# A diffusion block's first modulation, from column sums to products with a spread SiLU row, and its Fourier blocks four products side by side

## The chip, the cores and the metric

The kernel runs on one core of a Trainium2 chip. The metric is the device time of one execution in microseconds (us), as the median of the runs of a kernel. TensorE is called PE here, VectorE DVE, ScalarE ACT, GpSimd POOL, and SyncE, which issues most of the loads and stores, SP. Each engine works through its own list of instructions in order; a later one never overtakes one that waits.

## What is computed

One layer over 2048 latent tokens of width 1024 and 256 context tokens. What matters here is its beginning:

```python
sh1, sc1, g1, sh2, sc2, g2 = split(silu(c) @ w_ada + b_ada)      # w_ada: 1024 x 6144
hx = rms_norm(x, norm1_g) * (1 + sc1) + sh1                       # 2048 x 1024
fx, qx, kx, vx = split(hx @ w_in)                                 # fx: 512 columns, "Fourier"
y_four = fourier_mix(fx)                                          # needs every token
gates = sigmoid(hx @ w_branch_gate)                               # 2048 x 2048
# then attention, gated merge, output projection, and the squared-ReLU MLP
```

A product in 32-bit precision is made of three PE products of halves: each operand is split in a high part and a low part, and high-high, high-low and low-high are added in one PSUM bank (`mm3`, line 80). From the second quarter of the tokens on the halves are 16-bit numbers, scaled by powers of two.

## The kernel before, in words

The tokens are worked on in quarters j = 0 to 3 of 512. The width of 1024 is cut in KT = 8 blocks k of 128 channels. Weights come in units of 256 columns. The list `seq` (line 724) orders the work on PE in pairs of units: first the two Fourier units f, then two gate units g, then query, value, key and gate units. In pair 0 the output of quarter j of a unit is two products of 24 matmuls each (`unit_T`, line 535: 8 blocks by 3 products of halves), with 512 tokens in the free direction. The results are written to DRAM (`put_T`, line 530). The instructions of every engine are put in order when the program is built, by a scheduler that is held to a certain order only where the code says `issue_after`.

**The modulation.** AB (line 134) holds for each block k one column of shifts and one of scales, with a channel on each partition. `ada_load` (line 265) brings, per block, 1 MB of w_ada: input channels on the partitions, 128 shift and 128 scale columns side by side. `ada_sum` (line 272) multiplies input block after input block by the SiLU of c (a number per partition, `sil`) and adds them on DVE: two scalings (L278), then multiply-adds (L280), then an addition of two partial sums (L281). For blocks from 2 on, DVE takes six of the eight input blocks (PE_K = 6, line 737) and PE the other two. `ada_cols` (line 284) then sums over the partitions by PE products with a column of ones (L292), and with `sil` for those two (L291); DVE adds the bias (L294) and applies the norm gain (L295).

**Quarter 0** is built with 32-bit halves, since the power of two by which hx is scaled (`norm_scale`, line 249) is known only when all eight blocks of AB are there. `load_x` (line 194) fetches 128 tokens, squares them (L203 on ACT, L201 on DVE), raises the mean to the power -1/2 on POOL (L175) and scales the tokens (L208, L206). `hx_k` (line 211) transposes a block of 512 tokens on PE (L217), evicts it twice on ACT with AB's columns as scale and bias (L220, L222: firstH and ht) and has DVE make the low half (L225). The loop at line 768 makes block k + 1 and then the 12 products of block k, four output banks side by side. The weights' 32-bit halves are made by `split_on` (line 88: L90, L93).

**Quarters 1 to 3.** `build` (line 227) does the same with 16-bit halves: transposes (L233), ht (L237 on DVE or L239 on ACT), high half (L240), low half (L241). `load_unit` (line 495) finds the norm of a weight unit (L504, L505, L510, L511 to L515) and makes its halves (L523, L524). In pair 0, `run_pair` (line 802) works quarter 1, 2, 3. Between the two units of a quarter it calls `first_tokens` (line 789, quarter 0's 32-bit halves into 16-bit ones: L796, L798, L799) and fetches, normalises and builds the next quarter. All four quarters of hx stay in SBUF, in four rooms of one tag (line 697). Beside later products, `tick` (line 473) steps through side work, the other columns of the modulation first, and `load_gains` and `load_rope` (lines 547 and 564) fetch norm gains and rotary tables, which POOL multiplies (L571).

The rooms are shared. In the beginning, the weights of modulation lie in rooms that later hold hx and the rotary tables.

Of the kernel before, what the change touches and what calls it, by code (L numbers as in the profile page):

```python
# [8 lines left out]
F32 = mybir.dt.float32  # L9
# [57 lines left out]
def dit_block(ctx: ExitStack, tc: tile.TileContext, a, out, taps=None, upto=9):  # L67
# [126 lines left out]
    def load_x(src, r0, name, xh=None, sq_on_dve=False, scale_on_dve=False):  # L194
        if xh is None:
            xh = pb.tile([128, D], F32, tag="xh", name=f"xh_{name}", bufs=5)
        load(xh, src[r0:r0 + 128, :])
        sq = pb.tile([128, D], F32, tag="xsq", name=f"xsq_{name}")
# [6 lines left out]
        if scale_on_dve:  # L205
            dve.tensor_scalar(out=xh, in0=xh, scalar1=rs, scalar2=None, op0=ALU.mult)  # L206
        else:
            act.activation(xh, xh, AF.Copy, scale=rs)  # L208
        return xh

    def hx_k(xhs, k, hx, ab, name, t_on_act=False):

        hH, hL = hx
        w = hH.shape[2]
        tp = tpp.tile([128, 512], F32, tag="tp", name=f"tp_{name}_{k}")[:, :w]
# [3 lines left out]
        t = pb.tile([128, 512], F32, tag="ht", name=f"ht_{name}_{k}", bufs=2)[:, :w]  # L219
        h_ = act.activation(hH[:, k, :], tp, AF.Identity, bias=bi, scale=sc)  # L220
        if t_on_act:
            act.activation(t, tp, AF.Identity, bias=bi, scale=sc)  # L222
        else:
            dve.tensor_scalar(out=t, in0=tp, scalar1=sc, scalar2=bi, op0=ALU.mult, op1=ALU.add)
# [24 lines left out]
    def norm_scale(ab, i, name):  # L249
# [13 lines left out]
        dve.tensor_scalar(out=ab, in0=ab, scalar1=hsc[:, 2 * i:2 * i + 1], scalar2=None, op0=ALU.mult)  # L263
# [20 lines left out]
    def ada_cols(dst, j, c0, gain, name, acc, wt=None, nk=KT):  # L284

        ps = adp.tile([128, 512], F32, tag="ad", name=f"ad{name}")
        for i in range(2):
            bs = slice(i * 128, (i + 1) * 128)

            for k in range(nk, KT):  # L290
                pe.matmul(ps[:, i:i + 1], wt[:, k, bs], sil[:, k:k + 1], start=(k == nk), stop=False)  # L291
            pe.matmul(ps[:, i:i + 1], acc[:, bs], ones[:, 0:1], start=(nk == KT), stop=True)  # L292
        b = 32 + c0 // 128
        dve.tensor_tensor(out=view(dst, j, [[8, 2]]), in0=ps[:, 0:2], in1=view(vecT, b, [[8, 2]]), op=ALU.add)  # L294
        dve.scalar_tensor_tensor(out=dst[:, 8 + j:9 + j], in0=dst[:, 8 + j:9 + j], scalar=1.0, in1=gain,  # L295
                                 op0=ALU.add, op1=ALU.mult)

    def side_work():
        for dst, d0, s0, g0, o in ((ABc, 0, 8, 16, "c"), (AB2, 3 * D, 0, 24, "m")):
            for k in range(KT):  # L300
                c0 = d0 + k * 128
                acc = ada_sum(ada_load(k + (8 if d0 else 0), f"{o}{k}"), s0, f"{o}{k}")
                yield
                ada_cols(dst, k, c0, vecT[:, g0 + k:g0 + k + 1], f"{o}{k}", acc)
# [385 lines left out]
    sp.dma_start(vec[0:8, :], a["c"].rearrange("o (k p) -> (o k) p", p=128))  # L690
    sp.dma_start(vec[8:16, :], a["c_ctx"].rearrange("(k p) -> k p", p=128))
    sp.dma_start(vec[16:24, :], a["norm1_g"].rearrange("o (k p) -> (o k) p", p=128))
    sp.dma_start(vec[24:32, :], a["norm2_g"].rearrange("o (k p) -> (o k) p", p=128))
    sp.dma_start(vec[32:80, :], b_ada.rearrange("o (k p) -> (o k) p", p=128))
# [1321 lines left out]
```

## Time and profile before

| what | us |
|---|---|
| median of 3 runs | 2602.69 (2600.85 to 2606.18) |
| the profiled execution's own time | 2595.27 |
| its span, first to last instruction | 2593.5 |
| PE busy in the span | 2509.0 |
| PE busy from 0 to 157.4 (up to the first gate product) | 122.48 |
| PE busy from 157.4 to 900 | 716.92 |
| PE busy from 900 to 1700 | 781.94 |
| PE busy from 1700 to the end | 887.70 |

The profile is of one execution. Busy times overlap between engines, and matmuls overlap with each other, so that a busy time is not a price. A row of the timeline has its start, its length, the engine, the line of the kernel, the operation with the tiles written and read, shapes, and in brackets how long the engine was idle before it and what ended that. An x and a number behind a row say how many instructions are merged in it. In the list of groups the mean length of one instruction follows the busy time.

### The profile page before, as it was taken

What the parts mean: (1) busy time and instruction counts of PE and PEld (TensorE: products, weight loads), DVE (VectorE), ACT (ScalarE), POOL (GpSimd) and SP (SyncE); (2) the same over time, 40 slices, a digit from 0 to 9 for tenths busy, and PEclk for the clock granted to TensorE, in tenths of its full rate; (3) what the DMA queues carried; (4) which work ended last, traced back from release to release, by engine and by line L of the source; (5) the groups of instructions that cost most, each with busy time, mean ns of one, the idle gap of its engine ahead of it and who ended that gap; (6) DMA issues with size and microseconds to landing.
All of it is one profiled execution on the core that took longest, in us unless ns stands there. A gap on an engine that the chain in (4) does not pass through costs nothing.

```text
span 2593.5 us, 42160 instructions
## 1 busy us (share of the span) xinstructions
PE 2509.0 (97%) x15842; PEld 1445.0 (56%) x15842; DVE 1800.7 (69%) x3735; ACT 1199.8 (46%) x2118; POOL 450.7 (17%) x561
## 2 busy tenths in 40 slices
PE   7899999999999899999999999999999999999999
PEld 5445666777655577786665444444444444444444
DVE  7656969655464788986775887979778534546367
ACT  5633255335644688983444655546360423223150
POOL 1200221012122456620000121121212000000000
PEclk9899999999999999999999999999999999999999
DMA  7465666545875576646667777776876433333334
GB/s 276 119 217 203 200 212 235 188 157 191 288 282 159 143 229 191 188 142 202 233 217 273 256 264 241 256 259 228 287 269 196 141 95 109 97 107 94 110 102 154
DMA packets 223125, 506.39 MB, mean 195 GB/s; under 512 B 31732, under 2 KB 85756, under 8 KB 207816
## 3 DMA queue, kind: packets, MB, share of 16 engines
q1 hardware_dynamic: 189960, 384.57, 45.8%
q0 software_dynamic: 26176, 87.90, 9.6%
q10 hardware_dynamic: 6784, 31.21, 3.6%
q8 instruction: 124, 2.03, 0.3%
q14 instruction: 81, 0.66, 0.1%
HBM read 366.22 MB, written 137.38 MB: 194 GB/s over the span
## 4 chain that ended last, share of the span: by engine, by line
PE 74%; DVE 9%; DMA 9%; ACT 4%; issue 3%; SPq 1%; POOL 1%; ACTq 0%; DVEq 0%; POOLq 0%
PE p L85 20%; PE pm L85 19%; PE ps_g L85 8%; PE po L85 6%; PE pua L85 3%; PE tp L1444 2%; PE ps_q L85 2%; PE ps_f L85 2%; DMA vt<-v 2%; PE ps_v L85 2%; PE pv L1458 2%; PE ps_k L85 2%; DMA w12m<-in_w_mlp 2%; PE pmf L1379 1%; DMA w12m<-in_w_mlp1t 1%
## 5 line engine op out<-in xcount | busy, mean ns | idle before, releaser
L85 PE MATMUL pm<-hc,wb 128*128 128x512 f16 x2688 | 582.6, 379 | 5.5 <-DVE u L1728 3.5
L85 PE MATMUL p<-wb,a 128*128 128x512 f16 x2688 | 581.9, 379 | 2.4 <-DVE X L1853 1.8
L85 PEld LDWEIGHTS <-wb 128*128 128x128 f16 x2688 | 263.0, 98 | 323.4 <-issue 7.2
L85 PEld LDWEIGHTS <-a 128*128 128x128 f16 x2688 | 263.0, 98 | 320.0 <-issue 3.2
L85 PE MATMUL ps_g<-hx,w_g 128*128 128x512 f16 x1536 | 343.7, 379 | 0.0
L1853 DVE SCALAR_TENSOR_TENSOR X<-p,msc,X 128x512 f32<-128x512 f32 x280 | 201.5, 747 | 157.8 <-PE p L85 139.3
L85 PEld LDWEIGHTS <-hx 128*128 128x128 f16 x2304 | 227.0, 99 | 39.3 <-issue 3.6
L85 PEld LDWEIGHTS <-w_g 128*128 128x128 f16 x1536 | 150.4, 99 | 165.4 <-issue 0.9
L85 PE MATMUL po<-wo,mH 128*128 128x512 f16 x512 | 152.4, 379 | 0.0
L1728 DVE TENSOR_TENSOR u<-pm,u 128x512 f32<-128x512 f32 x128 | 87.4, 689 | 84.3 <-PE pm L85 82.5
L404 ACT ACTIVATE wo<-ws,msc 128x512 f16<-128x512 f32 x96 | 69.0, 719 | 161.4 <-DVE ws L446 130.2
L1732 ACT ACTIVATE p<-pm 128x512 f32<-128x512 f32 x32 | 18.9, 589 | 239.3 <-PE pm L85 239.3
L1431 DVE CUSTOM_DVE_ANT_0 s<-sc,bt,qsc 128x736 f32<-128x736 f32 (+5 forms) x128 | 111.2, 869 | 21.3 <-PE sc L1425 15.6
L1452 DVE SCALAR_TENSOR_TENSOR pL<-tp,pH 128x640 f16<-128x640 f32 (+1 forms) x128 | 112.4, 878 | 11.4 <-ACT pH L1447 10.7
L1864 POOL DMA_DIRECT2D xr<-x1d x32 | 17.2, 538 | 569.7 <-DVE X L1728 562.8
L1435 ACT ACTIVATE s<-s,m 128x736 f32<-128x736 f32 (+5 forms) x128 | 104.6, 817 | 15.1 <-DVE m L1431 15.0
L532 ACT ACTIVATE ot_g<-ps_g,usc_g 128x512 f32<-128x512 f32 x64 | 43.7, 683 | 146.2 <-PE ps_g L85 139.4
L1444 PE MATMUL tp<-ident,s 128*128 128x128 f32 x704 | 102.5, 280 | 4.1 <-ACT s L1435 3.9
L404 ACT ACTIVATE wo<-raw,msc 128x512 f16<-128x512 f32 x128 | 87.8, 710 | 38.1 <-DVE raw L446 17.0
L405 DVE SCALAR_TENSOR_TENSOR wo<-raw,msc,wo 128x512 f16<-128x512 f32 x128 | 94.3, 746 | 10.7 <-ACT wo L404 10.6
L85 PE MATMUL po<-wo,mL 128*128 128x512 f16 x256 | 97.0, 379 | 0.0
L1447 ACT ACTIVATE pH<-tp 128x640 f16<-128x640 f32 (+1 forms) x128 | 95.9, 749 | 0.5 <-PE tp L1444 0.5
(574 smaller groups left out, 4376.3 us busy)
## 6 DMA issues: line engine op xcount, KB each, us to landing
wb<-w1d SPq DMA_DIRECT2D x224, 256.0 KB
wb<-w2d SPq DMA_DIRECT2D x224, 256.0 KB
raw<-in_w_mlp ACTq DMA_DIRECT2D x24, 1024.0 KB
w1d<-wo POOLq DMA_DIRECT2D x84, 256.0 KB, 3.8
w2d<-wo POOLq DMA_DIRECT2D x84, 256.0 KB, 4.0
gT<-ot_g SPq DMA_DIRECT2D x64, 256.0 KB
w12m<-in_w_mlp1t SPq DMA_DIRECT2D x16, 1024.0 KB
w12m<-in_w_mlp SPq DMA_DIRECT2D x16, 1024.0 KB
```

What stands on the lines that cost most here:

```text
L85: last_mm[0] = pe.matmul(ps, l, r, start=(start and i == 0), stop=(stop and i == n - 1))
L404: act.activation(hi, src, AF.Copy, scale=scale)
L405: dve.scalar_tensor_tensor(out=lo, in0=src, scalar=scale, in1=hi, op0=ALU.mult, op1=ALU.subtract)
L532: last_out[0] = act.activation(o, ps, func, scale=scale)
L1431: tail["dve"] = dve.tensor_tensor_reduce(out=s[:, :n], in0=sc, in1=bias, op0=ALU.add, op1=ALU.min, scale=qsc[:, 4:5], scalar=3.0e38, accum ...
L1435: tail["act"] = act.activation(s[:, :n], s[:, :n], AF.Exp, bias=m1[:, 0:1], scale=-1.0, accum_out=m1[:, 1:2])
L1444: tail["pe"] = pe.transpose(tp[:, i * 128:(i + 1) * 128], s[:, o:o + 128], ident)
L1447: tail["act"] = act.activation(pH[:, :c], tp[:, :c], AF.Copy, scale=PTOP)
L1452: tail["dve"] = dve.scalar_tensor_tensor(out=pL[:, :c], in0=tp[:, :c], scalar=PTOP, in1=pH[:, :c], op0=ALU.mult, op1=ALU.subtract)
L1458: tail["pe"] = pe.matmul(pv, p_[:nk, i * 128:(i + 1) * 128], vv[:nk, h2 * 128 + o:h2 * 128 + o + 64], start=(j == 0 and i == 0), stop=(j = ...
L1728: last["dve"] = dve.tensor_tensor(out=o, in0=x, in1=y, op=op)
L1853: last["dve"] = dve.scalar_tensor_tensor(out=X[x], in0=ps, scalar=down if op == ALU.subtract else up, in1=X[x], op0=ALU.mult, op1=ALU.add)
```

## The change

- **The first modulation.** w_ada's first 2048 columns also come transposed (`w_ada_t`): an output channel on each partition, its 1024 weights along the lane, shift and scale side by side, 1 MB per block as before. ACT spreads `sil` to 1024 columns, PE transposes it in eight pieces and ACT copies it back, so that every partition has the whole SiLU row (`silb`). `first_channels` now needs two DVE instructions per block that multiply a lane by that row and sum (the profile's name of such an instruction is that of L201), each with a short read of the sum, and the two small ones on AB. Column sums on PE are gone for this modulation. The other modulations keep them, with another order of columns.
- **The start.** One load of a packed `vec` takes the place of five. The four x tiles of quarter 0 are fetched ahead of modulation block 0; `load_x` is parted in `x_fetch` and `x_norm`. The tokens of quarter 1 lie in rooms of their own (`x1_rooms`), those of quarter 3 in rooms that the SiLU row and a first weight half leave.
- **The order in pair 0.** The f weights' norms and high halves are made beside the first products (`f_norm`, `f_part`). `quad` makes a quarter's four products side by side, block after block, 12 matmuls each, in all four PSUM banks. hx of the next quarter (`steps`) and quarter 0's 16-bit halves (`first_tokens`) are made block by block beside it. hx has a named room for each quarter; quarter 3's is the one that held quarter 0's 32-bit low halves, and quarter 0's halves are made in the rooms of the modulation and copied by two DMAs of 1 MB into the room of its 32-bit high halves.

The core of the diff:

```diff
+    silw = silb[:, D:2 * D].rearrange("p (k n) -> p k n", n=128)
+    with tc.issue_after(exp_.ins):
+        spread_ = act.activation(silw, view(sil, 0, [[1, KT], [0, 128]]), AF.Copy)
...
+        for k in range(4):
+            pe.transpose(ps[:, k * 128:(k + 1) * 128], silw[:, 4 * h + k], ident)
+        with tc.issue_after(scaled[0].ins):
+            act.activation(silb[:, h * 512:(h + 1) * 512], ps, AF.Copy)
...
     def first_channels(k):
-        if k + 1 < KT:
-            first_sums(k + 1)
-        ada_cols(AB, k, k * 128, vecT[:, 16 + k:17 + k], f"s{k}", sums[k], first_ada[k], PE_K if k > 1 else KT)
-        made.append(hx_k(xhs, k, hx32, AB, "00", True))
...
+        with after(chan[-1], made[k - 2][1]) if k > 1 else nullcontext():
+            acc = pb.tile([128, 2], F32, tag="acc2", name=f"acc{k}", bufs=2)
+            for o in range(2):
+                w = first_ada[k][:, o * D:(o + 1) * D]
+                dve.tensor_tensor_reduce(out=w, in0=w, in1=silb[:, 0:D], op0=ALU.mult, op1=ALU.add, scale=1.0, scalar=0.0, accum_out=acc[:, o:o + 1])
+            dve.tensor_tensor(out=view(AB, k, [[8, 2]]), in0=acc, in1=view(vecT, 32 + k, [[8, 2]]), op=ALU.add)
...
+    def steps(j, room, xh):
+        hx[j] = room = room or hx_room(j, f"hx{j}")
+        for k in range(KT):
...
+            if k % (2 if j == 1 else 4):
+                dve.tensor_scalar(out=t, in0=tp, scalar1=sc, scalar2=bi, op0=ALU.mult, op1=ALU.add)
+            else:
+                act.activation(t, tp, AF.Identity, bias=bi, scale=sc)
+            edge["act"] = act.activation(room[:, 0, k], t, AF.Copy)
+            edge["dve"] = dve.tensor_tensor(out=room[:, 1, k], in0=t, in1=room[:, 0, k], op=ALU.subtract)
+            yield
...
+        hx[0] = room = hx_room(2, "hx0")
+        for o in range(2):
+            sp.dma_start(room[:, o].rearrange("p k t -> p (k t)"), r[o].rearrange("p k t -> p (k t)"))
+        yield
...
+    def quad(j, beside):
+        units = list(zip(f_w, f_usc))
+        ps = [mmp.tile([128, 512], F32, tag="mm", name=f"ps_f{m}_{j}") for m in range(4)]
+        for k in range(KT):
+            for m in range(4):
+                w, ms = units[m // 2][0], slice((m % 2) * 128, (m % 2 + 1) * 128)
+                mm3(ps[m], [(w[:, 0, k, ms], w[:, 1, k, ms], hx[j][:, 0, k], hx[j][:, 1, k])], k == 0, k == KT - 1)
+            beside(k)
         for m in range(4):
+            put_T(ps[m], fT, m, j * 512, AF.Copy, f"f{m}_{j}", units[m // 2][1][:, 1:2], o=f_room(m, f"ot_f{m}_{j}"))
...
+        def beside2(k):
+            if k == 0:
+                norm_quad(3, x_last)
+            if k < 3:
+                next(tokens)
+                next(tokens)
+            if k == 3:
+                for _ in tokens:
+                    pass
+            if k >= 4:
+                next(b3)
+                next(b3)
```

How the instructions stand now, at two places. On DVE, in the middle of the modulation, before: `aaccs` are the partial sums, `ads` PE's column sums, `sparec` and `sparer` rooms of w_ada.

```order
L278 TENSOR_SCALAR aaccs_344<-sparec,sil 128x256 x2
L280 SCALAR_TENSOR_TENSOR aaccs_344<-sparec,sil,aaccs_344 128x256 x2
L294 TENSOR_TENSOR AB<-ads_352,vecT 128x2
L280 SCALAR_TENSOR_TENSOR aaccs_344<-sparec,sil,aaccs_344 128x256 x2
L295 SCALAR_TENSOR_TENSOR AB<-AB,vecT 128x1
L281 TENSOR_TENSOR aaccs_344<-aaccs_344 128x256
L278 TENSOR_SCALAR aaccs_383<-sparer,sil 128x256 x2
L280 SCALAR_TENSOR_TENSOR aaccs_383<-sparer,sil,aaccs_383 128x256 x3
L225 TENSOR_TENSOR firstL<-ht_3_366,firstH 128x512
```

The same engine and place now, `ISA` being the product with a sum and, with 128x1, the reading of the sum; rooms 153 to 156 are named `hx_room` from the start.

```order
L773 ISA hx_room_153,acc_315<-hx_room_153,silb 128x1024
L773 ISA acc_315 128x1
L773 ISA hx_room_153,acc_315<-hx_room_153,silb 128x1024
L773 ISA acc_315 128x1
L229 TENSOR_TENSOR hx_room_156<-ht_2_293,hx_room_155 128x512
L774 TENSOR_TENSOR AB<-acc_315,vecT 128x2
L775 SCALAR_TENSOR_TENSOR AB<-AB,vecT 128x1
L773 ISA sparer,acc_376<-sparer,silb 128x1024
L773 ISA acc_376 128x1
```

AB of a block now follows its sums on the same engine, where before it took them from PE one block later.

On ACT, from the outputs of the quarter 1 products (`ot_f`) to the first high half of quarter 2 (`hx_822`), before; `xh` are quarter 2's tokens.

```order
L532 ACTIVATE ot_f_0_734<-ps_f_0_709,usc_f_592 128x512
L532 ACTIVATE ot_f_1_762<-ps_f_1_737,usc_f_592 128x512
L532 ACTIVATE ot_f_0_920<-ps_f_0_895,usc_f_608 128x512
L203 ACTIVATE xsq_784,ss_785<-xh_782 128x1024
L532 ACTIVATE ot_f_1_948<-ps_f_1_923,usc_f_608 128x512
L203 ACTIVATE xsq_794,ss_795<-xh_792 128x1024
L208 ACTIVATE xh_782<-xh_782,rs_789 128x1024
L208 ACTIVATE xh_792<-xh_792,rs_799 128x1024
L203 ACTIVATE xsq_1015,ss_1016<-xh_1013 128x1024
L208 ACTIVATE xh_1013<-xh_1013,rs_1020 128x1024
L239 ACTIVATE ht_0_828<-tp_0_823,AB 128x512
L240 ACTIVATE hx_822<-ht_1_837 128x512
```

On ACT now, from the outputs of quarter 2 (`ot_f_2`) to the first high half of quarter 3 (`hx_1002`); `t_4` to `t_7` and `h0H` are quarter 0's last blocks.

```order
L534 ACTIVATE ot_f_2_1119<-ps_f_2_873,usc_f_356 128x512
L534 ACTIVATE ot_f_2_1122<-ps_f_2_874,usc_f_356 128x512
L897 ACTIVATE h0H<-t_4_943 128x512
L534 ACTIVATE ot_f_2_1125<-ps_f_2_875,usc_f_366 128x512
L897 ACTIVATE h0H<-t_5_948 128x512
L534 ACTIVATE ot_f_2_1128<-ps_f_2_876,usc_f_366 128x512
L895 ACTIVATE t_6_965<-hx_room_156,hsc 128x512
L895 ACTIVATE t_7_970<-hx_room_156,hsc 128x512
L897 ACTIVATE h0H<-t_6_965 128x512
L897 ACTIVATE h0H<-t_7_970 128x512
L883 ACTIVATE ht_0_1008<-tp_0_1003,AB 128x512
L884 ACTIVATE hx_1002<-ht_0_1008 128x512
```

The next quarter's squares and scalings no longer stand behind the outputs, but quarter 0's last blocks do, and ahead of these twelve rows stand two norms of gate weights, with t_4 and t_5 between them.

More of the change, by code (lines that the diff above doesn't have):

```diff
@@ L282, in ada_sum, with ada_cols @@
         return acc[:, 0, :]
-    def ada_cols(dst, j, c0, gain, name, acc, wt=None, nk=KT):
+    def ada_cols(dst, i, d0, g0, name, acc):
         ps = adp.tile([128, 512], F32, tag="ad", name=f"ad{name}")
[L287 to L296, printed above, removed]
+        for h in range(2):
+            pe.matmul(ps[:, h:h + 1], acc[:, h * 128:(h + 1) * 128], ones[:, 0:1], start=True, stop=True)
+        scale, j = i < 4, 2 * (i % 4)
+        o = dst[:, 8 + j:10 + j] if scale else dst[:, j:j + 2]
+        b = 32 + d0 // 128 + (8 if scale else 0) + j
+        dve.tensor_tensor(out=o, in0=ps[:, 0:2], in1=vecT[:, b:b + 2], op=ALU.add)
+        if scale:
+            dve.scalar_tensor_tensor(out=o, in0=o, scalar=1.0, in1=vecT[:, g0 + j:g0 + j + 2], op0=ALU.add, op1=ALU.mult)
     def side_work():
@@ new lines, in dit_block @@
+    ada_rooms = [wide[i][:, o:o + 2048] for i in (1, 0) for o in (0, 2048)]
+    ada_rooms.append(pb.tile([128, 2, 16, 64], F32, tag="rcos", name="sparer").rearrange("p o t d -> p (o t d)"))
+    ada_rooms += ada_rooms[:3]
+    silb = pb.tile([128, 2, KT, C], F16, tag="hc", name="silb").bitcast(F32).rearrange("p o k t -> p (o k t)")
+    def first_load(k):
+        load(ada_rooms[k], a["w_ada_t"][k])
+        return ada_rooms[k]
+    w_in = a["w_in"]
+    w_g = a["w_branch_gate"]
+    raw_f = [pa.tile([128, KT, 256], F32, tag="wst", name=f"ws_f{u}", bufs=2) for u in range(2)]
@@ L780, in dit_block @@
[L780 to L800 removed]
+            with after(*made[1]):
+                first_half(1)
@@ new lines, in dit_block @@
+        if k == 2:
+            for i in range(5, 8):
+                first_ada[i] = first_load(i)
+            xh = [x_fetch(x2, (4 + i) * 128, f"01{i}", x1_rooms[i // 2][:, i % 2 * D:(i % 2 + 1) * D]) for i in range(4)]
+            x_late = fetch_quad(2)
+        first_products(k)
+        if k == 2:
+            with after(*made[3]):
+                for u in range(2):
+                    f_norm(u)
+        if k in (4, 5):
+            with after(made[k][0]):
+                f_part(k - 4, False)
@@ new lines, in dit_block, with f_room @@
+    x_last = fetch_last()
+    ordered[0] = False
+    for i, t in enumerate(xh):
+        with after(*made[5 if i < 2 else 6]):
+            x_norm(t, f"01{i}", i == 3, i == 3)
+    with after(norm_scale(AB, 0, "x"), made[7][1]):
+        f_part(0, True)
+    for u in f_usc:
+        dve.tensor_tensor(out=u[:, 1:2], in0=u[:, 5:6], in1=hsc[:, 1:2], op=ALU.mult)
+    def f_room(i, name):
+        if i % 2:
+            return pb.tile([128, 2, 512], F16, tag="s" + "HL"[i // 2], name=name, bufs=2).bitcast(F32).rearrange("p a t -> p (a t)")
```

237 lines of the change are left out of this document (155 added, 82 removed).

## The prediction

> **What bounds the kernel now.** First the page, for the share of each engine.
>
> ```profile
> span 2593.5 us, 42160 instructions
> ...
> PE 2509.0 (97%) x15842; PEld 1445.0 (56%) x15842; DVE 1800.7 (69%) x3735; ACT 1199.8 (46%) x2118; POOL 450.7 (17%) x561
> ```
>
> TensorE (PE) is busy for 97% of the span, so only its idle time can be won, and most of that lies where the change is made. The view by windows shows it for the stretch up to the first gate product. Its columns are the window, its length, then busy time and instructions of each engine, granted clock, DMA share and GB/s.
>
> ```profile
> 0.00:10.00 10.00, 0.37 (x1) 0.18 (x1) 3.21 (x12) 2.55 (x4) 1.00 (x11) 1.00 0.64 238
> 10.00:20.00 10.00, 3.77 (x12) 2.09 (x12) 4.63 (x13) 8.93 (x13) 3.19 (x4) 1.00 1.03 403
> 20.00:58.00 38.00, 36.74 (x199) 31.44 (x199) 33.86 (x94) 18.86 (x26) 4.77 (x5) 0.96 0.72 288
> ...
> 87.00:101.00 14.00, 4.97 (x18) 3.04 (x19) 7.79 (x16) 10.05 (x15) 4.70 (x5) 0.59 0.19 67
> ...
> 124.00:137.00 13.00, 6.91 (x43) 4.23 (x42) 11.27 (x19) 7.63 (x11) 10.58 (x5) 1.00 1.02 297
> ...
> sum 157.51, PE 122.59 PEld 76.19 DVE 109.53 ACT 88.30 POOL 29.59; mean PE 13.62 PEld 8.47 DVE 12.17 ACT 9.81 POOL 3.29
> ```
>
> PE is idle for 157.51 - 122.59 = 34.9 us there: 15.9 before 20 us, 9.0 in 87 to 101, 6.1 in 124 to 137. The list of PE's waits names the last two and part of the first:
>
> ```profile
> PE tp L233 <- ACT xh L208: 7.6, 2, 6.4
> PE ads L292 <- DVE aaccs L281: 6.9, 1, 6.9
> ...
> PE ps_f L85 <- DVE hx L241: 4.2, 1, 4.2
> ```
>
> The middle row is the start (the first column sum), the first is the token block of quarter 2, normalised only after quarter 1's outputs, the third quarter 3's block, late on VectorE (DVE). Between 20 and 58 PE looks busy but runs 96 exact products and 32 transposes in 37 us. The PE timeline (start, length, instruction) gives the marks against which I count:
>
> ```profile
> 20.34 2.07 PE L85 MATMUL ps_first<-firstH,w_first 128*128 128x512 f32 x4 [0.92 <-ACT firstH L220]
> ...
> 62.56 1.04 PE L85 MATMUL ps_f<-hx,w_f 128*128 128x512 f16 x4 [1.36 <-ACT w_f L523]
> ...
> 83.67 2.75 PE L85 MATMUL ps_f<-hx,w_f 128*128 128x512 f16 x12
> ...
> 136.98 4.00 PE L85 MATMUL ps_f<-hx,w_f 128*128 128x512 f16 x10 [4.25 <-DVE hx L241]
> ...
> 157.37 2.97 PE L85 MATMUL ps_g<-hx,w_g 128*128 128x512 f16 x13
> ```
>
> So the first products start at 20.3, quarter 1 runs from 62.6 to 86.4, and gate products begin at 157.4. From the gate products on, PE's list is the same products in the same order in both kernels: what is won or lost before 157.4 is the forecast, provided that nothing behind it waits anew.
>
> **The start.** One vector load replaces five, and the four x tiles stand ahead of the first modulation load.
>
> ```profile
> 0.72 0.40 SPq L690 DMA_DIRECT2D vec<-in_c  x1
> ...
> 2.18 0.32 SPq L694 DMA_DIRECT2D vec<-in_b_ada  x1
> ...
> 3.95 0.37 PE L711 MATMUL pvec<-ident,vec 80*128 80x80 f32 x1 [3.95 <-DMA vec<-in_b_ada]
> ...
> 5.37 0.17 DVE L717 TENSOR_TENSOR sil<-e,vecT 128x16 f32<-128x16 f32 x1
> ```
>
> The last of the five was taken 3.95 - 2.18 = 1.8 us after its issue, so the single one is there at 2.5 and the SiLU at 4.1 (5.54 - 3.95 = 1.6 later). In the chain of waits the first modulation block (1 MB) came 5.05 us after its issue:
>
> ```profile
> 2.54 5.05 DMA spare<-in_w_ada
> ```
>
> At the 403 GB/s of 10 to 20 us 1 MB takes 2.6, so 2.45 of it is latency. In the new order x tiles land at about 5.0, 6.3, 7.6, 8.9, modulation block 0 at 11.5, the first weight halves at 12.8 and 14.1, and then 2.6 us for each modulation block (the last at 34.8, before its turn). The prices of what is done with them, from the list of groups (count, busy us and mean ns, idle before):
>
> ```profile
> L241 DVE TENSOR_TENSOR hx<-ht,hx 128x512 f16<-128x512 f32 x24 | 16.8, 725 | 2.7 <-ACT hx L240 2.6
> ...
> L240 ACT ACTIVATE hx<-ht 128x512 f16<-128x512 f32 x24 | 14.4, 627 | 3.4 <-DVE ht L237 3.2
> ...
> L208 ACT ACTIVATE xh<-xh,rs 128x1024 f32<-128x1024 f32 x8 | 9.1, 1143 | 5.0 <-POOL rs L175 4.9
> ...
> L280 DVE SCALAR_TENSOR_TENSOR aaccs<-spare,sil,aaccs 128x256 f32<-128x256 f32 x20 | 8.4, 479 | 0.0
> ...
> L203 ACT ACTIVATE xsq<-xh 128x1024 f32<-128x1024 f32 x7 | 7.4, 1050 | 6.1 <-DMA xh<-in_x 6.1
> ...
> L220 ACT ACTIVATE firstH<-tp,AB 128x512 fp32r<-128x512 f32 x8 | 6.2, 776 | 18.2 <-DVE AB L295 18.1
> ...
> L201 DVE CUSTOM_DVE_ANT_0 xsq<-xh 128x1024 f32<-128x1024 f32 x5 | 6.1, 1225 | 0.2 <-DMA xh<-in_x 0.2
> L225 DVE TENSOR_TENSOR firstL<-ht,firstH 128x512 fp32r<-128x512 f32 x8 | 5.5, 688 | 0.3 <-ACT ht L222 0.3
> ...
> L93 DVE TENSOR_TENSOR w_first<-ws_f,w_first 128x1024 fp32r<-128x1024 f32 x4 | 4.9, 1222 | 3.1 <-ACT w_first L90 3.1
> ...
> L504 ACT ACTIVATE usq_f<-ws_f 128x2048 bf16<-128x2048 f32 x2 | 3.8, 1910 | 0.9 <-DVE ss L201 0.9
> ```
>
> A mean overlaps its neighbour by about 0.1, so I count 1.05 for a square, 1.1 for a scaling or a half of weights, 0.55 for a 512-wide copy, 1.9 for a weight norm. ScalarE (ACT): spread 4.1 to 5.2, two squares, two scalings, two copies of the row, 11.0. DVE: two squares and two scalings of x, 11.7; two product-sums (no such shape with the spread row stands in the trace; the nearest is L201, same size, 1225 ns, and I take that) 2.45 and two small ones 0.4: channel block 0 at 14.6. ACT's second weight half ends at 15.1, firstH 0.78 later: first product at **15.9**, 4.4 us sooner. The spread and its eight transposes cost PE nothing, since it idles there.
>
> **The eight channel blocks.** Before, one cost DVE two scalings, four L280 (six in the first two) and an addition, 0.6 + 4 x 0.42 + 0.4 = 2.7, with firstL 3.3; then came column sums on PE between its products, and DVE again: that trip is why ACT's L220 waited 18.1 us for AB. Now it is 2.45 + 0.4 + 0.62 for firstL = 3.5 on DVE, a little more, but without the trip. Block 1 comes late, behind two low halves (1.22 each) and firstL: 14.6 + 2.45 + 0.6 + 2.9 = 20.6. Block 2 waits for ACT's two evictions, firstL and the other two low halves: 28.4. Then 31.9, 35.4, 39.0, and with the small operations of the weight norm and the scale between them 43.0 and 46.8. Before, the last stood at 54.5:
>
> ```profile
> 54.50 0.16 DVE L295 SCALAR_TENSOR_TENSOR AB<-AB,vecT 128x1 f32<-128x1 f32 x1
> ```
>
> **Quarter 1.** From block 5 (39.0) on, ACT's queue is the bound, since squares and weight halves now stand between the evictions: 1.45 (evictions of block 5) + 2.1 + 2.2 + 1.45 + 1.1 + 1.05 + 1.45 + 2.2 + 2.2 ends at 54.2, then ht 0.7, hx 0.55, DVE's low part 0.7, and some 1.0 for semaphores: quarter 1 at **57.2**. That is 5.4 sooner than 62.6, but it runs without the early waits: the chain has 43 products in 9.30 us (0.216 each) and eight transposes in 0.87.
>
> ```profile
> 75.85 9.30 PE ps_f L85 x43
> ...
> 100.76 5.60 PE ps_f L85 x20
> 106.36 0.87 PE tp L233 x8
> ```
>
> 96 x 0.216 = 20.8, eight groups of four transposes 3.5, waits 0.7: end at **82.2** (86.4 before).
>
> **Quarter 2** starts at once: hx of blocks 0 and 1 is built inside quarter 1, and the four banks are emptied as they end. The 14 us hole from 87 to 101 goes. Its products end at 82.2 + 20.8 + 2.6 = 105.6.
>
> **Quarter 3** is what is late next, and by ACT's queue. The transposes of blocks 6 and 7 stand after 39 products of quarter 2, so ACT has its last hx of quarter 2 at 82.2 + 12.0 = 94.2. Behind it, in order and ahead of quarter 3's first hx, stand two squares (2.1), two scalings (2.2), two norms of gate weights (3.8), the six copies t_2 to t_7 and six h0H of quarter 0 (6.6), and the four outputs of quarter 2 (2.2): 16.9, with 0.7 for DVE between t_7 and h0H. Then ht, hx and DVE's low part, 1.9: quarter 3 at **113.7**, so PE stands for 8 us. It starts cold: 20 products took 5.60 after the old hole, 1.3 above 20 x 0.216. Its end: 113.7 + 20.8 + 2.2 (five groups of transposes) + 1.3 + 1.0 (gate weights beside hx on DVE) = **139.0**. The old stall of 4.25 there goes, because the multiplication of the rotary tables on POOL, which stretched w_g's low half to 3.21, now stands behind quarter 3's steps.
>
> ```profile
> 130.16 2.22 DVE w_g L524
> 132.45 3.21 DVE w_g L524
> ```
>
> **The clock.** After 4.25 us of idling ten products took 4.00 us where 2.16 is the warm price, after the hole of 87 to 101 the granted clock was 0.59. The Trainium skill (TensorE: Matmul & The Clock Gate, What's actually happening) says that the clock halves after an idle window of about 3.4 us. By that rule the pause of about 3 us ahead of quarter 1, which I price at nothing, stands at the limit, and the sum would be up to 1.8 us later there.
>
> **The new copy.** hx of quarter 0 goes by two DMAs of 1 MB from one SBUF room to another. No such copy is in the trace. From below it is the 2.6 us per MB above; from above the slowest load of the stretch:
>
> ```profile
> 121.70 7.65 DMA rsin<-in_sin
> ```
>
> That is 512 KB, so 31 us for both. Issued at 112, the copy lands between 117 and 143, and gates need it at 139. I take 122, nearer to the loads with long rows, whose shape it has; the far end costs 4. SP's queue has the loads of context modulation behind it; their sums are first read 10 us into the gates.
>
> **Sum.** 157.4 - 139.0 = 18.4, taken as 18. The profiled execution took 2595.27 us (span 2593.5 and 1.8 around it) and would take 2577; it lies 7.4 below the median of the runs, 2602.69, so the median would be **2584.7**.
>
> **Rivals.** (1) Quarter 3 doesn't wait: ACT gets through sooner than its order tells, the 8 us go too, 26 won, 2576.7. For it: half of the queued work is short; against: 16.9 us of counted rows stand there. Chance 0.12. (2) ACT falls behind already at blocks 5 to 7, where two squares and four weight halves stand between evictions, and each quarter starts 4 to 5 us later than counted, with the copy's far end beside it: 9 won, 2593.7. Chance 0.18. (3) Nothing is kept: loads of later stages that end waits come no sooner than now, so the span stays, 2602.7. Against it: those loads are queued behind work that moves too. Chance 0.07. (4) Slower: the copy of quarter 0 holds SP's queue and PE's gates. It decides once the copy takes more than 45 us (112 to 157.4), 1.5 times the far end; at 55 us gates start at 167, 2612. Chance 0.05. My forecast has 0.58.
>
> **Range and chances.** A measurement of this kernel tells about 0.2%, 5.2 us, from no change. Forecast with its unknowns (4 for the copy, 2 for loads, 3 for ACT) and rivals (1) and (2) reach from 2575 to 2595; (3) and (4) stay outside. Faster 0.88, same 0.07, slower 0.05.
>
> **What would show it.** First product at 16, AB's last column at 47, quarter 1 at 57 and 82, no hole behind it, a stall of 8 us ended by ACT or DVE ahead of quarter 3, gates at 139, and the same PE busy time from there on. Wrong would be gates later than 150, a wait of gates for the copy, or a product-sum far from 1.2 us.

## The result and the profile after

The changed kernel takes 2583.1 us (median of 4 runs, 2581.2 to 2584.81), the kernel before 2604.39 on the same chip: a ratio of 0.992, with a 95% interval of 0.9903 to 0.9937. The forecast was 2584.7.

The page of the changed kernel, for the share of each engine:

```profile
span 2582.7 us, 41995 instructions
...
PE 2506.0 (97%) x15770; PEld 1439.3 (56%) x15770; DVE 1798.2 (70%) x3710; ACT 1205.9 (47%) x2130; POOL 452.7 (18%) x561
```

Nothing stands out there, as before. The view by windows shows the stretch up to the gates; the columns are those of the prediction (window, length, busy time of PE, PEld, DVE, ACT, POOL, granted clock, DMA share, GB/s).

```profile
20.00:46.00 26.00, 21.23 (x95) 16.56 (x93) 23.75 (x63) 17.96 (x24) 4.49 (x4) 0.93 0.85 340
46.00:60.00 14.00, 12.27 (x59) 7.88 (x60) 11.28 (x22) 13.09 (x19) 2.19 (x2) 1.00 0.84 297
60.00:84.00 24.00, 24.00 (x129) 13.05 (x128) 17.36 (x30) 16.83 (x26) 3.89 (x4) 1.00 0.66 183
84.00:108.00 24.00, 20.17 (x106) 10.53 (x103) 14.54 (x25) 18.40 (x28) 5.26 (x6) 0.96 0.22 77
108.00:116.00 8.00, 4.74 (x15) 2.79 (x16) 6.95 (x10) 4.70 (x8) 0.00 (x0) 0.50 0.68 264
```

DVE is busy for 23.75 of the 26 us from 20 to 46, so that it may well pace the eight channel blocks (an experiment below asks). From 46 to 60 ACT is the fuller queue, with 13.09 of 14 us. From 60 to 84 PE never stands: the old 14 us hole is gone. What is left is the pair of lines at the end, PE idle around 104 to 111 with the granted clock at 0.50 behind it. The list of PE's waits up to 165 us names it first:

```profile
PE tp L877 <- ACT ht L883: 7.7, 2, 7.1
PE ps_first L85 <- ACT hx_room L227: 7.3, 3, 4.0
```

And the PE timeline gives the marks that answer to those of before (first product, quarter 1, the block ahead of quarter 3, quarter 3, gates):

```profile
17.46 2.07 PE L85 MATMUL ps_first<-hx_room,w_first 128*128 128x512 f32 x4 [2.86 <-ACT hx_room L227]
...
56.43 3.64 PE L85 MATMUL ps_f<-hx_room,w_f 128*128 128x512 f16 x16
...
111.26 0.48 PE L877 MATMUL tp<-ident,xh 128*128 128x128 f32 x1 [7.10 <-ACT ht L883]
...
112.17 1.91 PE L85 MATMUL ps_f<-hx,w_f 128*128 128x512 f16 x4
...
137.46 10.52 PE L85 MATMUL ps_g<-hx,w_g 128*128 128x512 f16 x48
```

| mark, us | before | forecast | after |
|---|---|---|---|
| first product | 20.34 | 15.9 | 17.46 |
| AB's last column | 54.50 | 46.8 | 45.15 |
| quarter 1 starts | 62.56 | 57.2 | 56.43 |
| PE's wait ahead of quarter 3 | 4.25 (inside it) | 8 | 7.10 |
| quarter 3 starts | | 113.7 | 112.17 |
| gates start | 157.37 | 139.0 | 137.46 |

The gates start 157.37 - 137.46 = 19.9 us sooner, and the medians differ by 21.3. Yet the two profiled spans differ by only 2593.5 - 2582.7 = 10.8 us. Behind the gates, where both run the same products, the first profile took 2593.5 - 157.37 = 2436.1 us, and this one 2582.7 - 137.46 = 2445.2. Two of the experiments ask which of these is the odd one.

### The profile page after: what moved, and what is told of

It is laid out like the page before. It is cut to its first block, busy times and chain, and to the rows that moved or that the text cites. A ratio compares the mean times of both kernels' runs of the same rounds, so it can differ in the third digit from the quotient of the medians.

```text
span 2582.7 us, 41995 instructions
## 1 busy us (share of the span) xinstructions
PE 2506.0 (97%) x15770; PEld 1439.3 (56%) x15770; DVE 1798.2 (70%) x3710; ACT 1205.9 (47%) x2130; POOL 452.7 (18%) x561
## 4 chain that ended last, share of the span: by engine, by line
PE 71%; DMA 10%; DVE 9%; ACT 5%; issue 3%; SPq 1%; POOL 0%; ACTq 0%; DVEq 0%; POOLq 0%
PE p L85 20%; PE pm L85 19%; PE ps_g L85 7%; PE po L85 5%; PE tp L1612 2%; PE ps_q L85 2%; PE ps_f L85 2%; PE ps_v L85 2%; PE pua L85 2%; DMA vt<-v 2%; DMA w12m<-in_w_mlp 2%; PE pv L1626 2%; PE ps_k L85 2%; PE pmf L1547 1%; DMA raw<-in_w_mlp 1%
## 5 line engine op out<-in xcount | busy, mean ns | idle before, releaser
L2021 DVE SCALAR_TENSOR_TENSOR X<-p,msc,X 128x512 f32<-128x512 f32 x280 | 201.2, 745 | 157.5 <-PE p L85 139.0
L85 PE MATMUL ps_g<-hx,w_g 128*128 128x512 f16 x768 | 173.4, 381 | 0.0
L85 PE MATMUL ps_g<-hx_room,w_g 128*128 128x512 f16 x768 | 172.0, 379 | 0.0
L85 PEld LDWEIGHTS <-hx 128*128 128x128 f16 x1152 | 113.8, 100 | 21.9 <-DVE vo_v L679 4.2
L85 PEld LDWEIGHTS <-hx_room 128*128 128x128 f16 x1152 | 114.4, 99 | 20.2 <-issue 3.0
L534 ACT ACTIVATE ot_g<-ps_g,usc_g 128x512 f32<-128x512 f32 x64 | 43.7, 683 | 138.2 <-PE ps_g L85 130.4
```

Source lines behind the costliest of these rows:

```text
L85: last_mm[0] = pe.matmul(ps, l, r, start=(start and i == 0), stop=(stop and i == n - 1))
L534: last_out[0] = act.activation(o, ps, func, scale=scale, bias=bias)
L2021: last["dve"] = dve.scalar_tensor_tensor(out=X[x], in0=ps, scalar=down if op == ALU.subtract else up, in1=X[x], op0=ALU.mult, op1=ALU.add)
```

## The experiments

Theory: the gain is what the marks say, 20 us ahead of the gates, from three parts (modulation without PE, x normalised early in rooms of its own, four products side by side), less a new wait that ACT's queue makes. Rivals: later stages give half of it back; ACT paces the start already; the copy of quarter 0 holds the gates; one of the parts does it all. All ratios below are to the kernel before, run on the same chip. The experiments ran on different chips, on which the kernel before took 2600.93 to 2604.39 us, so ratios compare better than medians. Where a wait is called none, no wait over 0.2 us stands there. The eighth is the kernel before itself (2602.54 us, one run).

| no., kernel | AB's last column | quarter 1 | wait ahead of quarter 3 | quarter 3 | gates | median | ratio, 95% interval |
|---|---|---|---|---|---|---|---|
| 1, changed, again | 44.11 | 55.63 | 7.1 | 111.38 | 136.09 | 2583.63 | 0.9929, 0.9917 to 0.9942 |
| 2, products written in turn | 44.80 | 56.01 | 8.1 | 112.75 | 137.67 | 2583.38 | 0.9931, 0.9917 to 0.9945 |
| 3, column sums | 56.54 | 63.46 | 5.3 | 118.46 | 143.28 | 2586.51 | 0.9948, 0.9931 to 0.9966 |
| 4, gate norms later | 45.28 | 56.78 | 4.4 | 110.72 | 135.43 | 2580.49 | 0.9924, 0.9908 to 0.9939 |
| 5, products forced in turn | 44.33 | 55.59 | none | 112.64 | 138.06 | 2588.32 | 0.9948, 0.9928 to 0.9968 |
| 6, x normalised late | 46.27 | 57.72 | 7.8 | 125.94 | 150.37 | 2596.89 | 0.9981, 0.9969 to 0.9992 |
| 7, norms later, quarter 0 earlier | 45.20 | 56.43 | 0.8 | 105.86 | 128.60 | 2573.59 | 0.9897, 0.9878 to 0.9916 |
| 9, copy twice | 45.40 | 57.18 | 7.1 | 113.78 | 138.54 | 2585.67 | 0.9937, 0.9921 to 0.9952 |
| 10, more work on DVE | 52.27 | 62.97 | 7.1 | 118.69 | 143.14 | 2587.27 | 0.9950, 0.9932 to 0.9968 |
| 11, weight halves later | 44.28 | 58.06 | 7.1 | 113.80 | 138.52 | 2586.56 | 0.9941, 0.9927 to 0.9956 |
| 12, the seventh, forced in turn | 44.37 | 55.66 | none | 114.37 | 144.46 | 2592.46 | 0.9964, 0.9951 to 0.9976 |

### Both kernels once more

No edit.

> The changed kernel unchanged, for a second profile. Behind the first gate product the two profiles run the same products in the same order, yet that stretch is 2593.5 - 157.37 = 2436.1 us before and 2582.7 - 137.46 = 2445.2 us after, so the profiled gain is 10.8 us where the gates start 19.9 sooner. Theory (the 9 us are the variation of single executions, whose granted clock differs by stretch): the second profile has gates at 137 to 138, a stretch of 2436 to 2446 behind them, and the median of the runs lies 18 to 23 below the median of the kernel before. Rival (later stages give 9 us back each time): again 2444 to 2446, the same new waits, and a median only 9 to 13 below.

> The kernel before unchanged, for a second profile. The stretch behind the first gate product was 2436.1 us in its first profile and 2440.5 to 2445.2 in the five profiles of the changed kernel and its variants, and that first profile was 7.4 us below the median of its runs. Theory (that execution was a fast one): now 2440 to 2446, gates at 157 to 158, a span near 2600. Rival (the later stages are 5 to 9 us slower in the changed kernel each time): 2434 to 2438 again.

The page and the PE timeline of the kernel before, second profile:

```profile
span 2600.7 us, 42160 instructions
...
155.98 1.24 PE L85 MATMUL ps_g<-hx,w_g 128*128 128x512 f16 x5
```

Behind the gates it now took 2600.7 - 155.98 = 2444.7 us, where the changed kernel's second profile took 2581.0 - 136.09 = 2444.9. So the first profile of before was a quick execution there. Over the fourteen profiles of this study the stretch lies between 2436.1 and 2448.3, with no tie to the edits that one profile of each can show (the second lowest, 2436.7, is that of the kernel with more work on DVE). With the second pair of profiles the gain is 2600.7 - 2581.0 = 19.7 of span and 155.98 - 136.09 = 19.9 at the gates: nothing is given back later, and the rival falls.

### The old column sums

```
-            dve.tensor_tensor_reduce(out=w, in0=w, in1=silb[:, 0:D], ..., accum_out=acc[:, o:o + 1])
+    sums.append(old_sum(first_ada[k], ...))      # DVE, 6 of 8 channel tiles from block 2 on
+    old_cols(k, ...)                             # PE: the other 2 and the sum over partitions
```

> Undoes the other part alone: the first modulation by column sums on DVE and PE as before, without the spread row, its transposes and the product-sums; quads, rooms and load order stay. Theory (the new sum takes out the trip to PE): first product at 19 to 21 instead of 17.5, AB's last column at 51 to 54 instead of 45.2, quarter 1 at 61 to 63 instead of 56.4, gates 4 to 6 later, time 4 to 6 above the changed kernel. Rival (DVE is the bound in both, 23.75 of 26 us busy from 20 to 46, and the column sums cost it less per block): AB's last column as early or earlier, time the same or up to 3 below.

The waits of PE show the trips back in the list (`ads` waits for DVE's partial sums) and the wait ahead of quarter 3 somewhat shorter:

```profile
PE tp L224 <- ACT xh L213: 6.8, 2, 5.6
PE tp L893 <- ACT ht L899: 5.3, 1, 5.3
PE ads L293 <- DVE aaccs L284: 2.7, 1, 2.7
```

Quarter 1 and the gates are 6 to 7 us later than in the changed kernel, as the theory had it. AB's last column came later still (56.54 where 51 to 54 was expected), and 2.0 later than the 54.50 of the kernel before. So the old sums fare worse in the new order than they did in the old one, and the 6.5 us that the new sum is worth here are perhaps more than it saves against the kernel before. The time tells less than the marks: the ratio is 0.0019 above that of the first experiment, 5 us, with intervals that overlap.

### Quarter 2's x normalised late

```
-        norm_quad(2, x_late)          # beside quarter 1, its steps from product block 4 on
         quad(1, beside1)
+        with after(last_out[0]):
+            norm_quad(2, x_late)
+        for _ in b2:
+            pass
         quad(2, beside2)
```

> Products side by side as in the changed kernel, but quarter 2's x is normalised behind quarter 1's outputs and its steps stand behind quarter 1, as in the kernel before. Theory (the 14 us hole was this order): PE stands 8 to 10 after quarter 1 (four outputs 2.2, two squares 2.1, POOL 1.5, two scalings 2.2, transposes and ht 1.5), quarter 2 ends at 113, ACT's last hx of quarter 2 is some 6 later than now, so the wait ahead of quarter 3 is 3 to 4 instead of 7: gates 5 to 7 later at 142 to 145, time 5 to 7 above the changed kernel. Rival (ACT's wait absorbs all of it): gates within 2.

PE's waits from 80 to 165 us:

```profile
PE tp L877 <- ACT ht L883: 8.5, 2, 7.8
PE tp L877 <- ACT xh L213: 5.2, 2, 4.0
```

The old wait for `xh` is back, quarter 2 starts at 93.06, and the wait ahead of quarter 3 is still 7.8. I had expected it to shrink to 3 or 4. It doesn't, because the steps for quarter 2's last blocks stand after some 40 products of quarter 2 in PE's list: when quarter 2 moves, ACT's last hx moves with it. The gates are 13 to 14 us later, about 1 of it because quarter 1 ended late in this profile (81.6 instead of 80.7, after a start with a cold clock). The ratio of 0.9981 is clear of the changed kernel's. With the 6.5 of the sums this comes near the 20, but the parts were taken out one at a time and act on each other, so that such a sum shows no exact split. No single part does it all.

### Four products in turn

First only written in turn, with k inside m:

```
-        for k in range(KT):
-            for m in range(4):
+        for m in range(4):
+            for k in range(KT):
```

> Undoes one part alone: the four products of a Fourier block run one after the other again (each over all 8 channel blocks), with x in its new rooms and the steps beside them at the same counts of products. Theory (side by side pays because a block's products need its channel blocks one by one): quarter 1's first product would need channel block 7, made at 70, where the unit would otherwise end at 62, quarter 2's needs blocks 4 to 7, made at 87 to 93, where it would end at 86, so 8 + 7 us and something in quarter 3, of which ACT's wait of 7 takes some back: gates at 147 to 155, time 10 to 18 above the changed kernel. Rival (the gain is the modulation and the rooms, the order of products hides nothing): within 3 us of the changed kernel.

The gates hardly moved (137.67), and PE's timeline says why. Quarter 1's first products stand there as in the changed kernel, 16 in a row:

```profile
56.01 3.64 PE L85 MATMUL ps_f<-hx_room,w_f 128*128 128x512 f16 x16
```

Behind them come groups of 12, 14, 5 and 14 with transposes between, in both kernels. So the scheduler kept the four products side by side, whichever loop stood outside. The run says nothing of the theory. So I bound the first matmul of each product behind the last of the one before:

```
+                with tc.issue_after(last_mm[0].ins) if m and k == 0 else nullcontext():
                     mm3(ps[m], ...)
```

> As the second experiment, but the first product of each of a block's four is bound behind the last of the product before it, so that PE's list really runs them in turn (written in turn alone, the compiled list ran them side by side again). Theory: quarter 1's first product needs channel block 7 (about 71) where its 24 would end at 62, so quarter 1 ends 7 to 9 later; quarter 2 and 3 wait for their blocks 4 to 7 some 3 to 5 each; ACT's wait of 7 gives back up to 5 of it. Gates at 146 to 154, time 8 to 15 above the changed kernel. Rival (the rooms alone do it): within 3.

Now the order on PE is another: quarter 1 begins with three products, and the next waits for the next block's hx.

```profile
55.59 0.83 PE L85 MATMUL ps_f<-hx_room,w_f 128*128 128x512 f16 x3
...
57.57 0.38 PE L85 MATMUL ps_f<-hx_room,w_f 128*128 128x512 f16 x1 [1.15 <-ACT hx_room L884]
```

PE's waits from 50 to 165 us are many and small, and the 7 us ahead of quarter 3 are gone (the 0.7 of the third row stands ahead of quarter 1):

```profile
PE ps_f L85 <- ACT hx_room L884: 2.6, 3, 1.1
PE ps_f L85 <- DVE hx_room L885: 1.7, 3, 1.1
PE tp L877 <- ACT ht L883: 0.9, 2, 0.7
```

Quarter 2's last product ends at 111.3 instead of 104, but quarter 3 starts at 112.64 instead of 112.17: ACT's ht was at 110.55, where it had been at 110.43. So the order of products saves 7 us there, and ACT's queue takes them back. The gates are 0.6 to 2.0 later than in the two profiles of the changed kernel, against the 9 to 18 that I expected. Whether the median's 5 us above it are real is open: the intervals overlap.

### What stands in ACT's queue

ACT's timeline of the changed kernel, from the gate weights' norms (L505) to quarter 3's first ht, has no gap over 0.21 us:

```profile
99.11 1.90 ACT L505 ACTIVATE usq_g<-ws_g 128x2048 bf16<-128x2048 f32 x1
100.91 0.19 ACT L505 ACTIVATION_READ_ACCUMULATOR usq_g<-ws_g 128x1 f32 x1
101.00 1.32 ACT L895 ACTIVATE t<-hx_room,hsc 128x512 f32<-128x512 f32 x2
102.23 1.90 ACT L505 ACTIVATE usq_g<-ws_g 128x2048 bf16<-128x2048 f32 x1
...
104.12 1.24 ACT L534 ACTIVATE ot_f<-ps_f,usc_f 128x512 f32<-128x512 f32 x2
...
108.98 1.29 ACT L897 ACTIVATE h0H<-t 128x512 f16<-128x512 f32 x2 [0.21 <-DVE t L896]
110.43 0.78 ACT L883 ACTIVATE ht<-tp,AB 128x512 f32<-128x512 f32 x1 [0.16 <-DVE h0L L898]
```

Quarter 2's outputs (L534) begin at 104.12, when PE has nothing left. Two things of that queue can stand elsewhere. First the norms:

```
             if k == 5:
+                with after(edge["act"]):     # behind quarter 3's first four hx
                     for o in new:
                         next(o)
```

> The two norms of gate weights (two squares of 2048 on ACT, 2.0 us each) stand behind quarter 3's first four hx instead of ahead of its first. Theory (the 7.1 us wait ahead of quarter 3 is ACT's queue): the wait falls to 3.0 to 3.5, quarter 3 starts at 108.5, gates at 133.5 to 134, time 3 to 4 below the changed kernel. Rival 1 (something else, x tiles or DVE, ends that wait next): the wait stays at 6 to 7, no change. Rival 2 (the gate weights are then late): the wait falls but PE waits 3 to 4 for w_g ahead of the gates, no change.

The wait fell from 7.1 to 4.4 us, by 2.7 where the norms' 4.0 were counted, and the gates don't wait for w_g. They start only 0.7 to 2.0 us sooner, because quarter 1 began late and with a cold clock in this profile (below), and the ratio (0.9924) can't be told from the changed kernel's. Then, with the same edit, quarter 0's halves in ACT's gaps between 78 and 91:

```
             if k >= 4:
                 next(b2); next(b2)
+                next(tokens)                 # beside quarter 1
-            if k < 3:                        # beside quarter 2: all six that are left
+            if k == 0:                       # only two
                 next(tokens); next(tokens)
```

> The norms of gate weights behind quarter 3's first hx as in the fourth experiment, and quarter 0's hx (t, h0H) spread into quarter 1's and early quarter 2's steps, where ACT idles 2.6 and 4.3 us. Theory (ACT's queue is that wait, whatever stands in it): the wait ahead of quarter 3 falls to 2 to 3.5, what is left being quarter 2's four outputs and ht, gates at 132 to 134, time 4 to 6 below the changed kernel. Rival (with the norms gone, the outputs of quarter 2 and the transposes set it): the wait stays at the 4.4 us of the fourth experiment and the time within 1 of it.

PE's waits from 80 to 165 us are one line, and quarter 3 starts warm (24 products in 5.34):

```profile
PE tp L877 <- ACT ht L883: 0.8, 1, 0.8
```

```profile
105.86 5.34 PE L85 MATMUL ps_f<-hx,w_f 128*128 128x512 f16 x24
...
128.60 3.62 PE L85 MATMUL ps_g<-hx,w_g 128*128 128x512 f16 x16
```

The gates start at 128.60, 8.2 us before the mean of the changed kernel's two profiles, where 3 to 5 were expected: quarter 3 starts 6.3 sooner than in the first of them, and from there to the gates takes 22.7 us instead of 25.3, with no cold start and fewer pauses. The ratio of 0.9897 (0.9878 to 0.9916) lies below that of the changed kernel's second measurement, whose interval it doesn't touch, and overlaps that of the first (0.9903 to 0.9937). The wait went from 7.1 over 4.4 to 0.8 us as work was taken out of ACT's queue, so that queue was the wait.

With that wait gone, the order of products can be asked once more, by the forcing edit of above on top of this kernel:

> The seventh experiment's kernel, with the four products of a block forced to run one after the other as in the fifth. In the changed kernel forcing them moved quarter 2's end from 104 to 111, but quarter 3 only from 112.2 to 112.6, since ACT was not ready before. Theory (what the order of products saves is hidden under ACT's wait, and shows once that wait is gone): quarter 2 ends at 110 to 112 instead of 104, PE hardly waits ahead of quarter 3, quarter 3 starts at 111 to 113 instead of 105.9, gates at 134 to 137 instead of 128.6, time 5 to 8 above the seventh experiment's kernel. Rival (the order of products is worth nothing here at all): gates within 2 of 128.6.

PE's waits from 50 to 165 us:

```profile
PE ps_f L85 <- ACT hx_room L884: 4.3, 4, 1.4
PE ps_f L85 <- DVE hx L885: 2.6, 2, 2.1
PE ps_f L85 <- DVE hx_room L885: 2.1, 4, 1.1
```

Quarter 3 starts at 114.37 instead of 105.86 and the gates at 144.46 instead of 128.60, 15.9 later, twice what I expected. Nearly half of it (7.4) stands inside quarter 3, whose first product now needs hx of blocks 4 to 7, and these stand on ACT behind the gate norms that the seventh experiment put there. That half belongs to the two edits together, not to the order of products alone. The time is 11.6 us below the kernel before on its chip, where the seventh's was 27.3 below on its own: 16 us apart, as the gates are, with intervals that don't touch. So four products side by side are worth much in that kernel, but in the changed kernel their worth lies under ACT's wait.

### The start

Does DVE pace it? One more pass for each block:

```
+                if o:
+                    dve.tensor_reduce(out=junk, in_=w, axis=AX.X, op=ALU.max, apply_absolute_value=True)
                 dve.tensor_tensor_reduce(out=w, in0=w, in1=silb[:, 0:D], ...)
```

> Each of the eight channel blocks gets one more pass of DVE over 1024 elements (a maximum that nobody uses, about 1.1 us), so 9 us of DVE before AB's last column. Theory (DVE's own work paces AB, and AB's last column quarter 1): AB's last column 7 to 9 later at 52 to 54, quarter 1 at 62 to 65, gates 6 to 8 later, time 6 to 8 above the changed kernel. Rival (ACT's queue is the bound from block 5 on, as the second rival of the prediction had it): AB 7 to 9 later, but quarter 1 only 2 to 4 and the time as much.

DVE's timeline there:

```profile
50.80 1.22 DVE L776 CUSTOM_DVE_ANT_0 hx_room<-hx_room,silb 128x1024 f32<-128x1024 f32 x1
...
52.27 0.16 DVE L778 SCALAR_TENSOR_TENSOR AB<-AB,vecT 128x1 f32<-128x1 f32 x1
```

AB's last column stands at 52.27, 7.1 later than in the first profile of the changed kernel, quarter 1 6.5 later and the gates 5.7 (8.2, 7.3 and 7.0 against the second profile). Most of what DVE gets to do in that stretch arrives at the gates. In the time it shows less: the median is 4 us higher, and the intervals overlap. The second rival of the prediction had quarter 1 4 to 5 us later than counted; it is out by the mark itself, since quarter 1 came 0.8 sooner than counted. But ACT's queue is a bound there too, as the prediction's own sum had it: in the changed kernel ACT has no gap over 0.2 us from 32.80 to 53.92, and takes block 7's firstH 3.2 us after AB's last column. So DVE is not the only pace.

And PE's wait of 4 us for block 2?

```
-        if k == 1:
-            with after(*made[1]):
+        if k == 2:
+            with after(*made[2]):
                 first_half(1)
```

> The split of the second weight halves (two of 1.0 us on ACT, two of 1.2 on DVE) stands one channel block later, behind block 2's evictions. Theory (PE's wait of 4 us for block 2's firstH is not on the path, since DVE's total work sets AB's last column): the wait falls to 1 to 2.5, block 2's first products start 2 to 3 sooner, AB's last column and quarter 1 within 0.7 of now, time within 2. Rival (that wait is on the path): quarter 1 and gates 2 to 3 sooner, time 2 to 3 below the changed kernel.

Block 2's products start at 27.65 instead of 30.46, and the wait is 1.44. AB's last column (44.28) lies between those of the changed kernel's two profiles (45.15 and 44.11), so it did not move: the wait was off the path to it, as the theory had it. Yet quarter 1 starts at 58.06, 1.6 to 2.4 later than in those profiles. ACT's order changed with the edit. In the changed kernel two weight halves (L822) stand behind block 7's firstH (L227):

```profile
48.33 0.76 ACT L227 ACTIVATE hx_room<-tp,AB 128x512 fp32r<-128x512 f32 x1
...
49.66 2.19 ACT L822 ACTIVATE w_f<-ws_f,usc_f 128x1024 f16<-128x1024 f32 x2
```

Here they stand ahead of it, and PE waits 1.85 us for it:

```profile
47.64 2.19 ACT L822 ACTIVATE w_f<-ws_f,usc_f 128x1024 f16<-128x1024 f32 x2
49.72 0.77 ACT L227 ACTIVATE hx_room<-tp,AB 128x512 fp32r<-128x512 f32 x1
```

So between AB's last column and quarter 1 it is ACT's list that counts.

### The copy of quarter 0

```
+            for _ in range(2):
                 sp.dma_start(room[:, o]..., r[o]...)
```

> The copy of quarter 0's hx from room to room is issued twice, and the second of each half waits in SP's queue for the first to land, so its issue shows that landing, and the loads of the context modulation stand behind it. Theory (1 MB takes about 2.6 us like the loads, and nothing waits for the copy): the second copies are issued at 114 to 118, all have landed by 125, gates at 136 to 138 and the time within 2 of the changed kernel. Rival (the copy goes at the price of the slow load, 15 us for 1 MB): second copies issued at 126 to 142, landed at 150 to 172, and PE waits 13 to 35 at the gates.

SP's queue: the second row pair waits for the first pair's landing.

```profile
111.91 0.56 SPq L903 DMA_DIRECT2D hx<-h0H  x1
112.64 0.49 SPq L903 DMA_DIRECT2D hx<-h0L  x1
116.50 0.47 SPq L903 DMA_DIRECT2D hx<-h0H  x1
119.32 0.47 SPq L903 DMA_DIRECT2D hx<-h0L  x1
```

1 MB had landed by 4.6 us after its issue, both by 7.4 (the theory had 2.6 for each, and the second issues by 118). The gates at 138.54 wait for nothing, even with the copy made twice. The fourth rival, which needed 45 us, is far off.

## Why the prediction was right, step by step

- **The start.** The forecast was 15.9, and 17.46 (16.68 in the second profile) was measured. The product-sum was priced at 1225 ns, and takes 1.22 us. What failed is the sum on DVE ahead of it, 11.7, as DVE's timeline shows:

```profile
8.63 1.22 DVE L206 CUSTOM_DVE_ANT_0 xsq<-xh 128x1024 f32<-128x1024 f32 x1 [0.93 <-DMA xh<-in_x]
...
9.96 1.22 DVE L206 CUSTOM_DVE_ANT_0 xsq<-xh 128x1024 f32<-128x1024 f32 x1
...
11.62 0.75 DVE L211 TENSOR_SCALAR xh<-xh,rs 128x1024 f32<-128x1024 f32 x1 [0.43 <-POOL rs L175]
...
13.10 0.75 DVE L211 TENSOR_SCALAR xh<-xh,rs 128x1024 f32<-128x1024 f32 x1 [0.66 <-POOL rs L175]
13.77 1.22 DVE L773 CUSTOM_DVE_ANT_0 hx_room<-hx_room,silb 128x1024 f32<-128x1024 f32 x1
```

  The third x tile was taken at 8.63, not 7.6 (7.85 in the second profile), and DVE's scalings wait for POOL's power, which the count left out. The first product-sum began 2.1 us late; 0.5 of it came back, since firstH had been counted behind a weight half on ACT that was done before AB.
- **The eight channel blocks.** AB's last column at 45.15 against 46.8. The price of 3.5 us per block on DVE held: (45.15 - 16.38) for seven blocks is 4.1, with the four low halves of weights (4.8) taken off 3.4. From the first block to the last the sum had 32.2 us where 28.8 passed, so the 1.8 that were lost at the start came back twice over (1.6 of it in the last two blocks, 6.2 against 7.8). That these two misses have opposite signs is luck. The experiment with more work on DVE confirms that DVE's work moves AB.
- **Quarter 1** at 56.43 against 57.2. ACT's queue, the bound of this step, ended at 53.92 against 54.2, and 2.5 us from there to the first product stand against 3.0, of which 1.0 "for semaphores" had no row behind it. Quarter 1's 96th product ends at 80.7 in the timeline, against 82.2. The waits of 0.7 between did not come.
- **Quarter 2** straight behind, PE's hole gone: right, and the late normalisation brings it back.
- **Quarter 3.** From ACT's last hx of quarter 2 (two from 91.44 to 92.8; forecast 94.2) to ht (110.43; forecast 94.2 + 16.9 + 0.7 = 111.8) are 17.6 us, as the queue was counted. From the end of PE's work before the wait to quarter 3's first product are 8.0 us (104.16 to 112.17) against 8.1, 7.10 of them the wait before the transposes. The first rival denied this wait; taking two kinds of work out of the queue took it away.
- **Gates** at 137.46 against 139.0, so 19.9 won against 18.4 counted. From quarter 3's start they took 25.3 us, as counted, the cold start included.
- **From span to median.** The forecast put the changed kernel's profiled execution at 2577; it took 2584.78. The profile of before was an unusually quick execution behind the gates (2436.1 us against 2444.7 the second time), so the offset of 7.4 did not carry over to another execution. The forecast stands because the saving was set against the median in the end. How close it came is partly luck: the medians differ by 21.3 us in the first measurement and by 17.9 in the second, with 18 forecast.
- **Not seen ahead:** that side-by-side products save next to nothing at the gates of this kernel (0.6 to 2.0 us in one profile), since the same ACT queue would have made quarter 3 wait anyway. The sum had no separate term for them, and so could not show it.

## What to carry to other kernels

Cost a reordering by the queue that ends last, not by the holes that it closes: here 7 us won at the end of quarter 2 were lost again to one engine's list, and moving two kinds of small work in that list won another 8 at the gates. When an experiment edits the written order, see in its trace whether the engine's order changed, and which other engine's order changed with it, before reading its time. And take two profiles of the kernel before: one execution can be off by more than the effect.

## What the runs showed of the hardware

- **The clock at the edge.** Between the exact products and quarter 1 PE runs only a few transposes for about 3.7 us (52.7 to 56.43). The same list came out warm or cold: 16 products took 3.64 us in the changed kernel, and 4.79, 4.85 and 4.50 in three others (norms later, x late, copy twice). The windows from 56 to 62 show the granted clock, first in the changed kernel:

```profile
56.00:62.00 6.00, 5.95 (x32) 3.01 (x31) 5.71 (x7) 5.09 (x9) 0.00 (x0) 1.00 0.86 223
```

  and where x is normalised late:

```profile
56.00:62.00 6.00, 5.66 (x23) 3.00 (x24) 5.44 (x7) 5.06 (x10) 0.00 (x0) 0.72 0.76 225
```

  The eight transposes just ahead were slow as well in the three. From the first of them to the end of the 16 products 6.23 us passed in all three, against 4.79 in the changed kernel, so the cold start costs 1.4 us, of the up to 1.8 that the prediction named. The Trainium skill (TensorE: Matmul & The Clock Gate, What's actually happening) has the clock halve after an idle window of about 3.4 us. This stretch has about that length, but PE was not idle in it, it ran 14 transposes; which way the clock falls here no run explains.
- **POOL beside DVE.** POOL's power of a 128x1 column took 0.55 us alone and 1.46 beside DVE's product of x with itself:

```profile
7.78 0.55 POOL L175 TENSOR_TENSOR rs<-ms,mhalf 128x1 f32<-128x1 f32 x1 [0.65 <-DVE ms L173]
10.13 1.46 POOL L175 TENSOR_TENSOR rs<-ms,mhalf 128x1 f32<-128x1 f32 x1 [1.80 <-DVE ms L173]
```

  The second spans 10.13 to 11.59, and the DVE instruction with two SBUF inputs 9.96 to 11.18. The Trainium skill (SBUF — State Buffer, Who interferes with whom) says that such an instruction contends with a GpSimd one that reads SBUF; the trace agrees. Of the 0.9 us, 0.43 show on the path to the first product, as DVE's idle time ahead of its scaling at 11.62.
